# Loading the early pairs' kept first products into the raw-data buffers, two early pairs ahead

## The chip, the cores and the metric

The kernel runs on one core of one Trainium2 chip. The metric is the device time of one execution in microseconds (us). TensorE is called PE here, and its weight loads PEld. VectorE is DVE, ScalarE is ACT, GpSimd is POOL and SyncE is SP. SP issues all DMAs of this kernel, one after the other, from one queue that is worked off in order; its own rows are marked SPq.

## The reference, cut to what matters

One decoder layer runs over 16 meta tokens and 1024 real tokens with a width of 2048. Its first step is a large projection, and the change lies within it:

```python
hs = jnp.concatenate([meta, x], axis=1)          # (1, 1040, 2048)
h = rmsnorm(hs, gain)
zin = h @ w_in                                   # (1040, 2048) @ (2048, 10240)
q, k, v, g_attn, u, g_pool, m_attn, m_pool = jnp.split(zin, cuts, axis=-1)
# attention on q, k, v, times silu(g_attn); pooling of u, times silu(g_pool); both projected up,
# weighted by sigmoid(m_attn) and sigmoid(m_pool), summed, projected by w_out, added to x, normed
```

All inputs and the output are float32.

## The kernel before, in words

**Seven products instead of eight.** `w_in` is taken in 40 pairs of 128-column blocks (`duos`, a pair is called `d`). For each pair the product of a 2 x 2 arrangement of blocks (two halves of the 2048 rows by the two column blocks) with a 2 x 2 arrangement of activations (two halves of the width by two halves of the tokens) is made from seven block products. Four of them are made in the first phase, with the activation operands `X0`, `X1`, `X2` and `X3`, which lie in SBUF; the other three follow in a later phase. The first product (weights `c0` of the upper half by `X0`) is needed three times: `X1`'s product is added to it in PSUM and gives a finished output (`out_c`), and its value alone, `s1`, is subtracted from the accumulator `b` of `X2` and of `X3` (`out_nu` on line 260 and `out_up` on line 265, both on DVE).

**One product, in pieces.** `block` takes one product for one `kq` (half of a half's rows): 4 k-chunks by 3 matmuls of 128x128 by 128x512. The three matmuls (lines 138, 139, 140) are hi by hi, hi by lo and lo by hi, since every float32 operand is split into a high part `wh` and a low part `wl` by `op_of`: ACT makes `wh` (line 116), then DVE makes `wl` (line 117). There are four buffers of each. A product is two such blocks, 24 matmuls.

**Raw weights and their sums.** `all_raws` issues four loads of 512 KB for a pair: `raws[0][0]`, `raws[0][1]`, `raws[1][0]`, `raws[1][1]`. There is room for one pair's raw weights only, so a load waits until the pair before has been read. `make_sums` adds raw blocks on POOL (line 236), eight additions per pair: `r1`, `r2`, `r3`, `r4` for each `kq`. `r2` and `r3` become the operands of `X2` and `X3`; `r1` and `r4` are stored to DRAM (`d_r`, line 245) for the later phase. The addition that comes first on POOL in most pairs needs `raws[1][0]`.

**Early pairs and rest pairs.** While the tokens are normed and turned, only `X0` and `X1` exist, so the first six pairs (`early`) get their `X0` and `X1` products there, and `s1` is written to DRAM (`d_nu`). When `X2` and `X3` stand, `early_rest(d)` does what is left of an early pair: it loads its four raws, loads `s1` back (line 417), makes the sums, then `X2`, `out_nu`, `X3`, `out_up`. The 34 other pairs (`rest`) do all four products at a stretch: `X0`, `X2`, `X1`, `X3`. After each of the first rest pairs one early pair is inserted (`more`): early 0, rest 0, early 1, rest 1, and so on to early 5, rest 5, then rest pairs alone. I call an early pair with the rest pair behind it a round.

**What sets the order.** A scheduler sets each engine's order from the program. A tile of a pool comes with as many buffers as its tag has, and an instruction that writes a tile waits until the tile that had the buffer is read. `s1` of an early pair is a tile of tag `st`, which has four buffers (`STB`) and is also used for each pair's `out_c`, `out_nu` and `out_up`. Tiles of tag `wr` (four buffers, `wr_tile`) hold raw data in the early phase and again, in this phase, from the seventh rest pair on (`fetch_x22`).

Of the kernel before, what the change touches and what calls it, by code (L numbers as in the profile page):

```python
# [72 lines left out]
def trunk_kernel(  # L73
# [14 lines left out]
    nc = tc.nc  # L88
# [12 lines left out]
    def dtile(name, shape):  # L101
        return dram.tile(list(shape), F32, tag=name, name=name)
# [8 lines left out]
    def nm(s):  # L111
        uid[0] += 1
        return f"{s}_{uid[0]}"
# [50 lines left out]
    d_nu = [dtile(f"d_nu{n}", (P, HALF)) for n in range(ND)]  # L164
# [29 lines left out]
    with ExitStack() as actx:  # L194
# [3 lines left out]
        def acc_tile():  # L198
            return psA.tile([P, 512], F32, tag="acc", name=nm("acc"), bufs=4)
# [10 lines left out]
        with ExitStack() as xctx:  # L210
# [3 lines left out]
            def load_raw(d, kh, kq, pool=None):  # L214
                if pool is None:
                    raw = ws.tile([P, QD, 2 * P], F32, tag=f"raw{kh}", name=nm("raw"), bufs=2 - kh)
                else:
                    raw = pool.tile([P, QD, 2 * P], F32, tag="rawb", name=nm("raw"), bufs=1)
                rows = krows(kh, kq)
                for c, w in ((0, 2 * P),) if d.c1 == d.c0 + P else ((0, P), (P, P)):  # L220
                    col = d.c0 if c == 0 else d.c1
                    nc.sync.dma_start(raw[:, :, c : c + w], w_in[rows, col : col + w].rearrange("(k p) c -> p k c", p=P))
                return raw

            def c0(raw):
                return raw[:, :, :P]
# [21 lines left out]
            def st_tile(pool, bufs):  # L248
                return pool.tile([P, HALF], F32, tag="st", name=nm("st"), bufs=bufs)
# [8 lines left out]
            def out_nu(pool, bufs, d, s1, b):  # L258
                t = st_tile(pool, bufs)
                nc.vector.tensor_tensor(out=t, in0=s1, in1=b, op=ALU.subtract)  # L260
                nc.sync.dma_start(d_nu[d.n], t)
# [22 lines left out]
            early = ALL[:6]  # L284
            ops = {}

            def wr_tile():
                return wp.tile([P, 512], F32, tag="wr", name=nm("wr"), bufs=4)
# [7 lines left out]
            with tc.tile_pool(name="px", bufs=1, side="right", reuse_waits="tile") as px:  # L296
# [82 lines left out]
                s1 = wr_tile()  # L379
# [11 lines left out]
                for d in early[1:]:  # L391
# [4 lines left out]
                    s1 = wr_tile()  # L396
# [10 lines left out]
            wa = xctx.enter_context(tc.tile_pool(name="wa", bufs=1, side="right", reuse_waits="tile"))  # L407
            SB = {"r1": 2, "r2": 2, "r3": 2, "r4": 2}
            STB = 4

            def all_raws(d):
                return [[load_raw(d, 0, 0), load_raw(d, 0, 1)], [load_raw(d, 1, 0), load_raw(d, 1, 1, wa)]]

            def early_rest(d):
                raws = all_raws(d)
                s1 = st_tile(wa, STB)
                nc.sync.dma_start(s1, d_nu[d.n])
                r2, r3 = make_sums(wa, d, raws, SB)
                b = acc_tile()
                for kq in range(KQ):  # L420
                    block([b], WHOLE, X2, kq, op_of(r2[kq]), True)
                out_nu(wa, STB, d, s1, b)
                for kq in range(KQ):
                    block([b], WHOLE, X3, kq, op_of(r3[kq]), False)
                out_up(wa, STB, d, s1, b)
# [30 lines left out]
                nc.sync.dma_start(d_tm, tm.rearrange("p a q k c -> p (a q k c)"))  # L456

            rest = ALL[len(early) :]
            early_rest(early[0])
            raws = all_raws(rest[0])  # L460
            r2, r3 = make_sums(wa, rest[0], raws, SB)
            for n, d in enumerate(rest):
                pieces = WITHM if d.meta else WHOLE
                a, b = [acc_tile() for _ in pieces], acc_tile()
                for kq in range(KQ):
                    block(a, pieces, X0, kq, op_of(c0(raws[0][kq])), True)
                s1 = copy_p1(wa, STB, a, pieces)
                for kq in range(KQ):
                    block([b], WHOLE, X2, kq, op_of(r2[kq]), True)
                out_nu(wa, STB, d, s1, b)  # L470
                for kq in range(KQ):
                    block(a, pieces, X1, kq, op_of(c0(raws[1][kq])), False)
                out_c(wa, STB, d, a, pieces)
                m7 = [op_of(r3[kq]) for kq in range(KQ)]
                last = d is rest[-1]
                more = n + 1 < len(early)
                if not last and not more:
                    raws = all_raws(rest[n + 1])
                    r2, r3 = make_sums(wa, rest[n + 1], raws, SB)
                for kq in range(KQ):  # L480
                    block([b], WHOLE, X3, kq, m7[kq], False)
                out_up(wa, STB, d, s1, b)
                if more:
                    early_rest(early[n + 1])
                    raws = all_raws(rest[n + 1])
                    r2, r3 = make_sums(wa, rest[n + 1], raws, SB)
                if 7 <= n < 7 + KC // 2:
                    second_operands(n - 7)
                if n == 7 + KC // 2:
                    second_meta()  # L490
                if 6 <= n < 6 + KC // 2:
                    fetch_x22(n - 6)
# [101 lines left out]
        with ExitStack() as a0ctx:  # L594
# [37 lines left out]
            for g, win in enumerate(WINDOWS):  # L632
# [4 lines left out]
                d = named["u", g]  # L637
# [35 lines left out]
        with tc.tile_pool(name="a1", bufs=1, side="right", reuse_waits="tile") as a1:  # L673
# [127 lines left out]
            for h in range(HEADS):  # L801
                d = named["kv", h]
# [228 lines left out]
```

## Time and profile before

| what | us |
|---|---|
| median of 3 runs (2631.22 to 2642.57) | 2633.88 |
| the profiled execution | 2634.98 |
| its span, from the first to the last instruction in the trace | 2633.2 |

The profile is of one execution. Its times count from the start of the span. A row of a timeline gives the start, the duration, the engine, the line, the tiles (out<-in, without buffer numbers), how many equal instructions are merged (x2), and in brackets for how long the engine had been idle before and what ended that. A row of waits gives who waited for whom, the total, how many times, and the longest. A matmul's duration overlaps with the next one's, so 0.39 us stands for matmuls that start every 0.227 us. PEclk is the share of full clock that TensorE was granted in a stretch: 1.00 is 2.4 GHz, 0.50 is 1.2 GHz.

### The profile page before, as it was taken

Reading aid. Unit: us, or ns where it says so; the run is one execution under the profiler, and the core shown is the slowest. Engines: PE = TensorE matmul, PEld = TensorE weight load, DVE = VectorE, ACT = ScalarE, POOL = GpSimd, SP = SyncE. Lnnn points to the kernel's source line nnn. Section 1 sums busy time; section 2 is a strip of 40 time slices with the busy share of each in tenths; the row PEclk is TensorE's granted clock in tenths of the full one; section 3 lists DMA queues with packets and bytes.
Section 4 is the critical chain, followed back from the end, with each engine's and each line's share of the span. In section 5 each row is a group of like instructions: output and inputs, shape, how many; then the busy total and the mean of one; then the engine's idle time right before and its main releaser. Section 6 shows DMA issues by size and latency. Waiting matters only on the chain.

```text
span 2633.2 us, 36249 instructions
## 1 busy us (share of the span) xinstructions
PE 2506.8 (95%) x12968; PEld 2139.4 (81%) x12968; DVE 1279.7 (49%) x2121; ACT 933.9 (35%) x1893; POOL 871.0 (33%) x794
## 2 busy tenths in 40 slices
PE   6878789999999999899999999999989999999998
PEld 5767678888888887888888888888778888788888
DVE  5433235553333335565676567656644324544432
ACT  6412122222222225223555455545532224322331
POOL 1654455554444543224333333333111101211010
PEclk8989899999999999999999999999999999999999
DMA  5565555556555557434344433442384434664431
GB/s 178 166 205 188 176 184 196 193 207 203 175 182 178 185 174 242 143 117 152 118 123 137 127 118 124 137 127 90 117 275 144 143 108 138 192 199 141 147 102 64
DMA packets 392053, 415.88 MB, mean 158 GB/s; under 512 B 29872, under 2 KB 264752, under 8 KB 390832
## 3 DMA queue, kind: packets, MB, share of 16 engines
q1 hardware_dynamic: 391872, 413.57, 49.5%
q8 instruction: 101, 1.65, 0.3%
q14 instruction: 80, 0.66, 0.1%
HBM read 302.62 MB, written 110.85 MB: 157 GB/s over the span
## 4 chain that ended last, share of the span: by engine, by line
PE 79%; DVE 5%; DMA 3%; POOL 2%; issue 2%; ACT 1%; SPq 0%; POOLq 0%; DVEq 0%; ACTq 0%
PE acc L138 16%; PE acc L139 16%; PE acc L140 16%; PE accb L140 4%; PE accb L138 4%; PE accb L139 4%; PE accb L903 4%; PE accb L901 4%; PE accb L902 4%; POOL r L236 2%; PE tr L721 1%; DMA raw<-in_w_in_dram 1%; DVE s L649 1%; DVE bt L706 1%; PE av L139 1%
## 5 line engine op out<-in xcount | busy, mean ns | idle before, releaser
L138 PE MATMUL acc<-x,wh 128*128 128x512 f32 (+2 forms) x2736 | 983.8, 360 | 57.2 <-DVE st L260 42.0
L140 PE MATMUL acc<-x,wl 128*128 128x512 f32 (+2 forms) x2736 | 972.4, 355 | 2.3 <-POOL wl L117 1.3
L139 PE MATMUL acc<-x,wh 128*128 128x512 f32 (+2 forms) x2736 | 972.7, 356 | 0.0
L138 PEld LDWEIGHTS acc<-x,wh 128*128 128x128 f32 x2736 | 521.9, 191 | 126.9 <-DVE st L260 44.4
L140 PEld LDWEIGHTS acc<-x,wl 128*128 128x128 f32 x2736 | 520.8, 190 | 75.8 <-DVE wl L117 2.7
L139 PEld LDWEIGHTS acc<-x,wh 128*128 128x128 f32 x2736 | 521.8, 191 | 63.8
L116 ACT ACTIVATE wh<-wr 128x512 fp32r<-128x512 f32 x480 | 302.4, 630 | 523.2 <-PE acc L139 165.7
L117 DVE TENSOR_TENSOR wl<-wr,wh 128x512 fp32r<-128x512 f32 x360 | 257.4, 716 | 279.1 <-ACT wh L116 268.4
L117 POOL TENSOR_TENSOR wl<-wr,wh 128x512 fp32r<-128x512 f32 x120 | 166.5, 1387 | 346.4 <-ACT wh L116 282.1
L117 DVE TENSOR_TENSOR wl<-r,wh 128x512 fp32r<-128x512 f32 x160 | 147.0, 922 | 254.4 <-ACT wh L116 254.4
L116 ACT ACTIVATE wh<-r 128x512 fp32r<-128x512 f32 x160 | 100.9, 632 | 445.1 <-PE acc L139 234.5
L236 POOL TENSOR_TENSOR r<-raw,raw 128x512 f32<-128x512 f32 x80 | 110.5, 1381 | 403.9 <-DMA raw<-in_w_in_dram 376.4
L236 POOL TENSOR_TENSOR r<-r,raw 128x512 f32<-128x512 f32 x160 | 225.5, 1410 | 13.3 <-DMA raw<-in_w_in_dram 3.4
L138 PE MATMUL accb<-x,wh 128*128 128x512 f32 x512 | 200.9, 392 | 9.5 <-ACT wh L116 9.5
L140 PE MATMUL accb<-x,wl 128*128 128x512 f32 x512 | 201.0, 393 | 3.0 <-DVE wl L117 3.0
L139 PE MATMUL accb<-x,wh 128*128 128x512 f32 x512 | 200.6, 392 | 0.0
L117 DVE TENSOR_TENSOR wl<-raw,wh 128x512 fp32r<-128x512 f32 x136 | 115.4, 856 | 141.8 <-ACT wh L116 140.1
L903 PE MATMUL accb<-wl,x 128*128 128x512 f32 x448 | 174.4, 389 | 1.0 <-DVE wl L117 1.0
L901 PE MATMUL accb<-wh,x 128*128 128x512 f32 x448 | 174.3, 389 | 0.0
L902 PE MATMUL accb<-wh,x 128*128 128x512 f32 x448 | 174.3, 389 | 0.0
L116 ACT ACTIVATE wh<-raw 128x512 fp32r<-128x512 f32 x160 | 99.3, 627 | 186.2 <-PE acc L139 146.9
L705 DVE TENSOR_TENSOR_SCAN wt<-wt 128x272 f32<-128x272 f32 (+5 forms) x128 | 107.6, 840 | 110.5 <-POOL wt L700 65.1
(164 smaller groups left out, 2979.7 us busy)
## 6 DMA issues: line engine op xcount, KB each, us to landing
raw<-in_w_in_dram SPq DMA_DIRECT2D x96, 512.0 KB, 5.2
d_r<-r SPq DMA_DIRECT2D x160, 256.0 KB, 2.0
wr<-d_r SPq DMA_DIRECT2D x160, 256.0 KB, 2.9
raw<-in_w_in_dram SPq DMA_DIRECT2D x152, 256.0 KB, 5.2
wr<-in_w_out_dram SPq DMA_DIRECT2D x128, 256.0 KB, 2.6
wr<-in_w_in_dram SPq DMA_DIRECT2D x80, 256.0 KB, 3.0
wr<-in_w_pool_up_dram SPq DMA_DIRECT2D x64, 256.0 KB, 3.8
wr<-in_w_attn_up_dram SPq DMA_DIRECT2D x64, 256.0 KB, 3.5
```

The costliest lines, as they stand in the source:

```text
L116: nc.scalar.activation(hi, src, AF.Copy)
L117: (eng or nc.vector).tensor_tensor(out=lo, in0=src, in1=hi.bitcast(F32), op=ALU.subtract)
L138: nc.tensor.matmul(ps, wh, rh, start=first, stop=False, skip_group_check=skip)
L139: nc.tensor.matmul(ps, wh, rl, start=False, stop=False, skip_group_check=skip)
L140: nc.tensor.matmul(ps, wl, rh, start=False, stop=last, skip_group_check=skip)
L236: nc.gpsimd.tensor_tensor(out=t, in0=a, in1=b, op=ALU.add)
L649: nc.vector.tensor_tensor(out=nxt[:, lo:], in0=cur[:, lo:], in1=cur[:, lo - sh : TOK - sh], op=ALU.add)
L705: nc.vector.tensor_tensor_scan(out=rev, data0=rev, data1=rev, initial=wt[:, w : w + 1], op0=ALU.mult, op1=ALU.bypass)
L706: nc.vector.tensor_tensor(out=bt[:, :w], in0=bt[:, :w], in1=wt[:, 1 : w + 1], op=ALU.mult)
L901: nc.tensor.matmul(a, sh, wh, start=k == 0, stop=False)
L902: nc.tensor.matmul(a, sl, wh, start=False, stop=False)
L903: nc.tensor.matmul(a, sh, wl, start=False, stop=k == KC - 1)
```

## The change

`s1` of an early pair no longer comes from tag `st` and is no longer loaded within `early_rest`. A new function `fetch_s1` takes a `wr` tile and loads `s1` into it. It is called for early 0 and early 1 ahead of the first `early_rest`, and for early n + 2 ahead of `early_rest` of early n + 1.

```diff
+            kept = {}
+
+            def fetch_s1(d):
+                kept[d.n] = wr_tile()
+                nc.sync.dma_start(kept[d.n], d_nu[d.n])
+
             def early_rest(d):
                 raws = all_raws(d)
-                s1 = st_tile(wa, STB)
-                nc.sync.dma_start(s1, d_nu[d.n])
+                s1 = kept.pop(d.n)
                 r2, r3 = make_sums(wa, d, raws, SB)
...
             rest = ALL[len(early) :]
+            fetch_s1(early[0])
+            fetch_s1(early[1])
             early_rest(early[0])
...
                 if more:
+                    if n + 2 < len(early):
+                        fetch_s1(early[n + 2])
                     early_rest(early[n + 1])
```

Only SP's order changes. PE, ACT and POOL have the same instructions in the same order, and on DVE `out_nu` and `out_up` of early pairs read a `wr` tile where they read an `st` tile.

SP before, where `s1` of early 1 is loaded. `d_r7` are the sums of rest pair 1 (pair 7), `d_up6` is a result of rest pair 0, and `raw_336` and `raw_337` are the last two raws of rest pair 1:

```order
L222 DMA raw_336_1863<-in_w_in_dram 128x4x256
L279 DMA d_sa6_94<-st_304_1720 128x512
L222 DMA raw_337_1865<-in_w_in_dram 128x4x256
L245 DMA d_r7_0_141<-r1_340_1871 128x512
L245 DMA d_r7_1_142<-r4_341_1873 128x512
L266 DMA d_up6_253<-st_309_1755 128x512
L417 DMA st_314_1766<-d_nu1_208 128x512
L245 DMA d_r7_0_141<-r1_344_1881 128x512
```

SP after, the place where the same load (`d_nu1`) stands now, among the stores of the sums of early 0 (`d_r0`):

```order
L461 DMA d_tm_391<-tm2_974_5068 128x256
L418 DMA wr_252_1488<-d_nu0_207 128x512
L398 DMA d_nu5_212<-wr_244_1441 128x512
L418 DMA wr_253_1490<-d_nu1_208 128x512
L245 DMA d_r0_0_127<-r1_260_1504 128x512
```

The load has moved past all of rest pair 0 and out from behind two stores of rest pair 1's sums. The loads for early 2 to 5 stand as early: that of early 5 stands in round 2.

SP before, in round 1 (early 1 with rest 1), the stores of early 1's sums (`d_r1`) and the raws of rest 1 (`raw_334` to `raw_337`):

```order
L245 DMA d_r1_0_129<-r1_317_1772 128x512
L222 DMA raw_334_1859<-in_w_in_dram 128x4x256
L245 DMA d_r1_1_130<-r4_318_1774 128x512
L261 DMA d_nu6_213<-st_299_1685 128x512
L245 DMA d_r1_0_129<-r1_321_1782 128x512
L222 DMA raw_335_1861<-in_w_in_dram 128x4x256
L245 DMA d_r1_1_130<-r4_322_1784 128x512
L222 DMA raw_336_1863<-in_w_in_dram 128x4x256
```

SP after, the same place (the raws are `raw_335` to `raw_338` here):

```order
L245 DMA d_r1_0_129<-r1_318_1774 128x512
L418 DMA wr_427_2300<-d_nu4_211 128x512
L222 DMA raw_335_1861<-in_w_in_dram 128x4x256
L245 DMA d_r1_1_130<-r4_319_1776 128x512
L261 DMA d_nu6_213<-st_300_1687 128x512
L245 DMA d_r1_0_129<-r1_322_1784 128x512
L245 DMA d_r1_1_130<-r4_323_1786 128x512
L222 DMA raw_336_1863<-in_w_in_dram 128x4x256
L222 DMA raw_337_1865<-in_w_in_dram 128x4x256
```

In this one round the second raw of the rest pair now stands behind the last store of the early pair's sums; in the later rounds it stands ahead of that store, as before.

SP after, between the sums of rest 3 (`d_r9`) and the raws of early 4 (`raw_486` to `raw_489`). The same kinds stand there before the change, with one more load (`s1` of early 3) ahead of the last two `d_r9`:

```order
L245 DMA d_r9_0_145<-r1_461_2423 128x512
L245 DMA d_r9_1_146<-r4_462_2425 128x512
L222 DMA raw_486_2572<-in_w_in_dram 128x4x256
L261 DMA d_nu3_210<-st_445_2363 128x512
L222 DMA raw_487_2574<-in_w_in_dram 128x4x256
L266 DMA d_up3_250<-st_450_2398 128x512
L222 DMA raw_488_2576<-in_w_in_dram 128x4x256
L222 DMA raw_489_2578<-in_w_in_dram 128x4x256
```

Before and after, all four raws of an early pair stand behind the last store of the rest pair's sums.

## Rows read from the trace of the kernel before

**Rows 1.** The page, busy time of each engine.
```profile
PE 2506.8 (95%) x12968; PEld 2139.4 (81%) x12968; DVE 1279.7 (49%) x2121; ACT 933.9 (35%) x1893; POOL 871.0 (33%) x794
```
**Rows 2.** Waits of all engines, 140 to 360 us (total, times, longest).
```profile
DVE st L260 <- DMA st<-d_nu: 46.9, 5, 12.6
...
PE acc L138 <- DVE st L260: 42.0, 5, 12.2
```
**Rows 3.** Timeline of SP, 225 to 245 us.
```profile
226.29 0.32 SPq L245 DMA_DIRECT2D d_r<-r  x1
...
227.13 0.45 SPq L417 DMA_DIRECT2D st<-d_nu  x1
```
**Rows 4.** Timeline of DVE, 120 to 420 us: the second of five such waits.
```profile
230.44 0.69 DVE L260 TENSOR_TENSOR st<-st,acc 128x512 f32<-128x512 f32 x1 [8.02 <-DMA st<-d_nu]
```
**Rows 5.** Busy time by stretch after five waits: first, sum (PEclk third from the end).
```profile
188.51:194.71 6.20, 6.20 (x15) 4.84 (x16) 1.04 (x2) 0.63 (x1) 0.10 (x1) 0.50 0.81 244
...
sum 26.01, PE 25.99 PEld 20.49 DVE 4.42 ACT 1.30 POOL 0.89; mean PE 5.20 PEld 4.10 DVE 0.88 ACT 0.26 POOL 0.18
```
**Rows 6.** Timeline of POOL, 140 to 450 us: first addition of some pairs.
```profile
140.31 1.27 POOL L236 TENSOR_TENSOR r<-raw 128x512 f32<-128x512 f32 x1 [4.59 <-DMA raw<-in_w_in_dram]
...
161.37 1.29 POOL L236 TENSOR_TENSOR r<-raw,raw 128x512 f32<-128x512 f32 x1 [8.95 <-DMA raw<-in_w_in_dram]
178.34 1.26 POOL L236 TENSOR_TENSOR r<-raw,raw 128x512 f32<-128x512 f32 x1 [6.13 <-DMA raw<-in_w_in_dram]
...
264.64 1.30 POOL L236 TENSOR_TENSOR r<-raw,raw 128x512 f32<-128x512 f32 x1 [6.15 <-DMA raw<-in_w_in_dram]
289.66 1.28 POOL L236 TENSOR_TENSOR r<-raw,raw 128x512 f32<-128x512 f32 x1 [14.70 <-DMA raw<-in_w_in_dram]
...
306.56 1.29 POOL L236 TENSOR_TENSOR r<-raw,raw 128x512 f32<-128x512 f32 x1 [4.93 <-DMA raw<-in_w_in_dram]
331.20 1.29 POOL L236 TENSOR_TENSOR r<-raw,raw 128x512 f32<-128x512 f32 x1 [13.85 <-DMA raw<-in_w_in_dram]
...
348.61 1.29 POOL L236 TENSOR_TENSOR r<-raw,raw 128x512 f32<-128x512 f32 x1 [5.41 <-DMA raw<-in_w_in_dram]
374.54 1.28 POOL L236 TENSOR_TENSOR r<-raw,raw 128x512 f32<-128x512 f32 x1 [15.16 <-DMA raw<-in_w_in_dram]
...
396.97 1.29 POOL L236 TENSOR_TENSOR r<-raw,raw 128x512 f32<-128x512 f32 x1 [10.09 <-DMA raw<-in_w_in_dram]
...
419.63 1.29 POOL L236 TENSOR_TENSOR r<-raw,raw 128x512 f32<-128x512 f32 x1 [10.34 <-DMA raw<-in_w_in_dram]
441.31 1.33 POOL L236 TENSOR_TENSOR r<-raw,raw 128x512 f32<-128x512 f32 x1 [10.16 <-DMA raw<-in_w_in_dram]
```
**Rows 7.** Waits of the DMA queue, 160 to 375 us.
```profile
SPq L222 <- DVE wl L117: 21.3, 13, 2.3
```
**Rows 8.** Busy time by stretch: the first phase after the last early pair.
```profile
365.38:1000.00 634.62, 634.62 (x3331) 549.58 (x3330) 266.00 (x336) 175.90 (x332) 314.80 (x224) 1.00 0.57 187
```
**Rows 9.** Timeline of DVE, 388 to 398 and 724 to 729 us: `wl` from `r2`.
```profile
389.29 0.68 DVE L117 TENSOR_TENSOR wl<-r,wh 128x512 fp32r<-128x512 f32 x1
...
726.11 1.22 DVE L117 TENSOR_TENSOR wl<-r,wh 128x512 fp32r<-128x512 f32 x1 [3.87 <-ACT wh L116]
```
**Rows 10.** Timeline of PE: the matmuls that first read these two `wl`.
```profile
397.09 0.39 PE L140 MATMUL acc<-x,wl 128*128 128x512 f32 x1
...
728.69 0.39 PE L140 MATMUL acc<-x,wl 128*128 128x512 f32 x1
```
**Rows 11.** Timeline of PE, 100 to 420 us: two shorter waits.
```profile
125.79 0.50 PE L138 MATMUL acc<-x,wh 128*128 128x512 f32 x1 [2.48 <-ACT wr L397]
140.96 0.50 PE L138 MATMUL acc<-x,wh 128*128 128x512 f32 x1 [2.38 <-ACT wh L116]
```
**Rows 12.** Busy time by stretch, after these two waits.
```profile
126.45:129.86 3.41, 3.41 (x10) 2.64 (x9) 0.59 (x1) 0.63 (x1) 2.57 (x3) 0.50 0.37 127
140.96:147.00 6.04, 5.55 (x23) 4.08 (x24) 3.56 (x4) 1.26 (x2) 4.94 (x5) 1.00 0.78 273
```

## The prediction, made before the changed kernel ran

> **What bounds the kernel now.** I read the page first. PE is busy for 2506.8 us, 95% of the span [rows 1], so a change pays only where PE waits, or where its clock is down. The waits of 140 to 360 us come next: PE waits 42.0 us in 5 pieces for DVE's line 260, and DVE's line 260 waits 46.9 us in 5 pieces for the load `st<-d_nu` [rows 2]. It is one chain with five links, one in each of rounds 1 to 5; the kernel has no larger wait of PE for one reason. The timeline of SP shows why the load is late: it is issued at 227.13 us, right behind the store of the rest pair's result and behind a store of the next rest pair's sums [rows 3], and DVE starts `out_nu` at 230.44 after 8.02 us of idling [rows 4]. The wait has a second price. In the busy time by stretch, the work that follows each of the five waits runs at a granted clock of 0.50, that is 1.2 GHz, for 26.01 us together [rows 5]; at 2.4 GHz it would take half, so 13.0 us are lost. At stake are thus 42.0 + 13.0 = 55 us, 2.1% of the run.
>
> Then I asked what arrives next once PE is not held there, and went to POOL's timeline. The first additions of the pairs [rows 6] are the clock of a second chain: raw loads, eight additions, stores, raw loads. From early 1's sums (161.37) to rest 6's (374.54) five rounds take 213.17 us, 42.6 each. The first leg, from an early pair's sums to its rest pair's, takes 16.97, 16.90 and 17.41 us where both ends are shown, mean 17.1. The second leg takes the rest: 25.02, 24.64 and 25.93 us. PE's own work in a round is 144 matmuls; with one started every 0.227 us that is 32.7 us, less than any round of POOL. So PE has room to be held by POOL's chain, and that decides how much of the 55 us is kept.
>
> **The wait that is removed.** After the change all six loads stand far ahead: that of early 1 among the stores of early 0's sums, the others as early. `out_nu` reads an operand that has landed more than a pair before. The 46.9 us of DVE and the 42.0 us of PE [rows 2] go as such; I see no way in which this load could still be late, since its buffer has stood idle since the early phase.
>
> **What is late next.** An early pair's raws stand in SP's order behind the last store of the rest pair's sums, before and after, and its sums need them; that is the second leg. How much of its 25.5 us is due to the stalled PE? The raw buffers of the rest pair are read by `wh` and `wl` too, whose four buffers PE empties, and the DMA queue waits 21.3 us in 13 pieces for `wl` [rows 7]. These waits go when PE is on time. What is left is seen once, in round 0, where `s1` was loaded long before it was needed: from 140.31 to 161.37, 21.06 us, 8.95 of it idle for a raw [rows 6]. Built up from pieces: the eight additions take 12.0 us where DVE is at work beside them (289.66 to 306.56 less 4.93 idle), the raw burst adds 8.95, and one store more than in round 0 (`out_nu`'s rows now reach DRAM in each round) some 0.6, an estimate of about a quarter of the burst's time for 512 KB below: 21.6. The pairs without early pairs between them give legs of 22.43, 22.66 and 21.68 us (374.54, 396.97, 419.63, 441.31). I take 21.6, nearest to the one row of the same order; the bounds are 19.7 (the row of 21.06 with faster additions, next paragraph) and 22.7.
>
> A row speaks against this. While DVE stood still, the eight additions took 289.66 − 264.64 − 14.70 = 10.3 us; while it worked, 12.0. So part of the stall was not lost: POOL ran faster in it by 1.7 us per round. That is inside my 21.6; at the old speed the sum below would be 5 x 1.7 = 8.5 us better. The Trainium skill, "SBUF — State Buffer", section "Who interferes with whom", states the rule that a DVE instruction with two SBUF inputs contends with a GpSimd instruction that reads SBUF; by that rule the slower additions come back as soon as DVE works on, and the rows agree in direction.
>
> The first leg doesn't hang on PE: the early pair's raws and sums run while PE still works on the pair before. I keep 17.1; its bounds are the lowest and highest row, 16.9 and 17.4.
>
> **What is added.** Each fetch moves 256 KB that was moved before too; nothing is issued more often. But two fetches more (of early 3 and 4) fall within the raw loads of round 1, and in that round the second raw of rest 1 now stands behind the last store of early 1's sums. One more raw then lands in the burst: 512 KB at the 273 GB/s of the stretch 140.96 to 147.00 [rows 12] is 1.9 us. I take 2.0 for both, bounds 0 (the loads hide in POOL's additions) and 2.9 (with another 256 KB). DVE reads `wr` where it read `st`: I put nothing, since shape and type stay (0.69 us [rows 4]); were it twice as long, ten instructions would add 7 us to DVE, which is busy for 49% [rows 1] and covers them. The `st` buffer that is set free lets stores of results go a little earlier, which nobody waits for after the change; if somebody does, it is a gain inside the range.
>
> **The sum.** A round takes 17.1 + 21.6 = 38.7 us, five take 193.5, with 2.0 for round 1 195.5. Against 213.2 POOL's chain is 17.7 us ahead when it begins rest 6, at about 357 instead of 374.5. PE would be free to be further ahead: its 55 us exceed that. It is held to POOL, in waits for `wh` of `r2` early in `X2` of the early pair: 38.7 − 32.7 − the remaining idle for other operands, some 3 to 4 us a round, in place of 8.4.
>
> **What is given back later.** From 365.38 to 1000.00 PE isn't idle for a moment, 634.62 of 634.62 [rows 8]. POOL's chain is ahead of PE there, but not by much and not ever more. For rest 6 `wl` of `r2` is made at 389.97 (389.29 + 0.68 [rows 9]) and first read at 397.09 [rows 10]: 7.1 us to spare. For a pair further on it is made at 727.33 [rows 9] and read at 728.69 [rows 10]: 1.36 us, the least I found. After the change PE comes to rest 6 with no time to spare, so it will be held to POOL's chain all through this phase, and the end of the phase moves by POOL's lead plus what was to spare where it was least: 17.7 + 1.4 = 19. Some raw loads of the rest pairs waited on DVE and so on PE; with PE closer they start a little earlier. For that I put 1 us (bounds 0 and 9, the second of which belongs to the first rival). **The gain is 20 us.** The profiled execution took 2634.98 us, 1.8 more than its span and 1.1 more than the median of 2633.88. So 2615 for a repeat of that execution, and **2614** against the median.
>
> **Rivals.**
> *POOL's chain is not the bound.* If its second leg shrinks with PE all the way and the later pairs give back nothing, the gain grows to 17.7 + 9 = 27 us (2607), and in the extreme to all 55 us (2579). For it: the DMA queue waits 21.3 us for `wl`, on PE's side [rows 7], and in the stall the additions went faster. Against it: the leg of 21.06 us came with `s1` in place, and the spare time of 1.36 us at 728 us doesn't grow because PE arrives sooner. Chance 0.17, time about 2605.
>
> *POOL's chain is slower than the one row.* With legs of 17.4 and 22.7, as in the slowest rows [rows 6], a round takes 40.1; with another 0.6 for the store 40.7. Five of them and 2.0 are 205.5, the lead is 7.7, with 1.4 to spare 9 us: 2625. For it: round 0 had no rest pair's results to store ahead of its raws. Against it: 22.66 was seen while PE had the time to be late. Chance 0.20.
>
> *Slower than before, through the clock.* PE would come into the 28 rest pairs behind round 5 with a short wait in each. The wait of 2.48 us at 125.79 [rows 11] was followed by 3.41 us at a clock of 0.50 [rows 12], which costs 1.7 us beside the wait; the wait of 2.38 us at 140.96 [rows 11] was followed by a clock of 1.00 [rows 12]. If every one of the 28 pairs had such a drop, 28 x 1.7 = 48 us would outweigh the 20: 2662; in every second pair the loss is 24 and the time 2638. It decides from 12 drops on. Against it: the hold per pair in that phase is the difference between POOL's leg and PE's own work, 96 matmuls or 21.8 us for a rest pair: at most 22.66 − 21.8 = 0.9 us, below both waits shown. Chance 0.05, 0.04 of it over the bound of a measurement.
>
> *The change doesn't do what it says*, some load being late all the same through SP's order: 2634, no change. Chance 0.03.
>
> **How the numbers follow.** The forecast has 0.55, the first rival 0.17, the second 0.20, the clock 0.05, no effect 0.03. Within the forecast the unknown terms give: second leg 19.7 to 22.7 (five times 1.9 better or 1.1 worse), round 1's burst 2.0 better or 0.9 worse, later phase 1 worse or 8 better. They don't come together; 10 better and 6 worse is fair. The range takes in the second rival and the near part of the first: 2602 to 2627. About 0.5%, 13.2 us, is what a measurement of this kernel can tell from no change, so faster means below 2620.7. The forecast is nearly all below that, the second rival nearly all above. Faster 0.78, same 0.18, slower 0.04.
>
> **What would show it.** Step one is right if PE's waits for line 260 are gone or below 2 us, and the fetches are issued a round or more ahead. Step two is right if POOL's first additions stand 38 to 39.5 us apart from round to round, with rest 6's near 357 us, and if PE has new waits of 2 to 5 us a round for ACT's `wh` of `r2`. If those waits are missing and POOL's legs are shorter than 21, the first rival holds; legs over 22.5 speak for the second. The later phase should show many small waits of PE, under 1 us each, at a clock of 1.00; a clock of 0.50 there is the third rival. The eight additions should take 12.0 us in the second leg also. A wait that I haven't seen, on another queue, would make all of it wrong: then PE's waits from 140 to 360 us would name another releaser.

## The result, and the profile after

The changed kernel takes 2604.58 us (median of 4 runs, 2601.93 to 2607.19) against 2633.57 us of the kernel before (median of 4). The ratio is 0.9884, 95% interval [0.9858, 0.9909]: 29 us faster, between 24 and 37. The forecast of 2614 us was 9 us too slow; the measured time lies inside the range, where the first rival stood (2605). The profiled execution took 2601.93 us with a span of 2600.2, 33.0 us less than the span before; that pair of executions lies somewhat further apart than the medians do.

The page, busy time of each engine, to hold against [rows 1]: PE has about as much work in a shorter span.

```profile
PE 2502.7 (96%) x12968; PEld 2132.8 (82%) x12968; DVE 1279.1 (49%) x2121; ACT 930.7 (36%) x1893; POOL 873.3 (34%) x794
```

Waits of the changed kernel from 140 to 360 us (total, times, longest), to hold against [rows 2]:

```profile
DVE st L260 <- PE acc L140: 16.1, 11, 1.8
PE acc L138 <- ACT wh L116: 13.5, 7, 3.6
```

DVE's wait for `st<-d_nu` and PE's wait for line 260 are gone from the list. What DVE's line 260 waits for now is PE, as it should be. PE's new wait is for `wh`, 13.5 us in 7 pieces, one of which, 3.6 us, lies ahead of the rounds: 9.9 us in 6 pieces are left for them.

The reason is seen in two rows of early 1: SP's timeline has the load at 126.71 us, ahead of all of rest pair 0, and DVE's has `out_nu` at 176.01 us, behind a wait for PE alone (compare [rows 4]).

```profile
126.71 0.42 SPq L418 DMA_DIRECT2D wr<-d_nu  x1
```
```profile
176.01 0.69 DVE L260 TENSOR_TENSOR st<-wr,acc 128x512 f32<-128x512 f32 x1 [0.77 <-PE acc L140]
```

POOL's timeline, first additions of early 1, rest 1, early 4, rest 4, early 5, rest 5 and rest 6, as in [rows 6]:

```profile
161.44 1.29 POOL L236 TENSOR_TENSOR r<-raw,raw 128x512 f32<-128x512 f32 x1 [8.55 <-DMA wr<-d_nu]
179.06 1.28 POOL L236 TENSOR_TENSOR r<-raw,raw 128x512 f32<-128x512 f32 x1 [6.78 <-DMA raw<-in_w_in_dram]
...
277.23 1.29 POOL L236 TENSOR_TENSOR r<-raw,raw 128x512 f32<-128x512 f32 x1 [9.74 <-DMA raw<-in_w_in_dram]
294.16 1.29 POOL L236 TENSOR_TENSOR r<-raw,raw 128x512 f32<-128x512 f32 x1 [6.13 <-DMA raw<-in_w_in_dram]
314.89 1.28 POOL L236 TENSOR_TENSOR r<-raw,raw 128x512 f32<-128x512 f32 x1 [9.74 <-DMA raw<-in_w_in_dram]
331.29 1.38 POOL L236 TENSOR_TENSOR r<-raw,raw 128x512 f32<-128x512 f32 x1 [5.62 <-DMA raw<-in_w_in_dram]
351.97 1.29 POOL L236 TENSOR_TENSOR r<-raw,raw 128x512 f32<-128x512 f32 x1 [9.63 <-DMA raw<-in_w_in_dram]
```

(The first row names the load of an `s1` as releaser, which is no operand of that addition; its idle time is near the 8.95 us of [rows 6].) Five rounds take 351.97 − 161.44 = 190.5 us instead of 213.2. The forecast had 195.5 and rest 6 at about 357.

Now the same two places in the later phase as in [rows 9] and [rows 10]: PE's matmuls that first read `wl` of `r2`, for rest 6 and rest 21, and DVE's instructions that made it.

```profile
366.02 0.39 PE L140 MATMUL acc<-x,wl 128*128 128x512 f32 x1
```
```profile
697.62 0.39 PE L140 MATMUL acc<-x,wl 128*128 128x512 f32 x1
```
```profile
362.59 1.22 DVE L117 TENSOR_TENSOR wl<-r,wh 128x512 fp32r<-128x512 f32 x1 [3.86 <-ACT wh L116]
...
695.04 1.22 DVE L117 TENSOR_TENSOR wl<-r,wh 128x512 fp32r<-128x512 f32 x1 [3.87 <-ACT wh L116]
```

This is the surprise. PE reads 397.09 − 366.02 = 31.07 us earlier for rest 6, and 728.69 − 697.62 = 31.07 us earlier for rest 21, to the hundredth the same. Nothing was given back. The time to spare is 366.02 − 363.81 = 2.2 us for rest 6, where it was 7.1, and 697.62 − 696.26 = 1.36 us for rest 21, the very value of before. The many small waits of PE that the prediction named as a sign are not there. The busy time by stretch says the same: from 344 to 965 us PE is never idle and its clock is 1.00 (third number from the end), as in [rows 8].

```profile
344.00:965.00 621.00, 621.00 (x3271) 538.20 (x3270) 261.34 (x327) 168.98 (x323) 314.44 (x224) 1.00 0.59 192
```

So 31 of the 33 us come from the rounds. The other 2 lie elsewhere in the run, where nothing was changed, and I did not follow them.

### The profile page after: what moved, and what is told of

The parts are those of the page before. It is cut to its first block, busy times and chain, and to the rows that moved or that the text cites. A ratio compares the mean times of both kernels' runs of the same rounds, so it can differ in the third digit from the quotient of the medians.

```text
span 2600.2 us, 36248 instructions
## 1 busy us (share of the span) xinstructions
PE 2502.7 (96%) x12968; PEld 2132.8 (82%) x12968; DVE 1279.1 (49%) x2121; ACT 930.7 (36%) x1893; POOL 873.3 (34%) x794
## 4 chain that ended last, share of the span: by engine, by line
PE 82%; DVE 5%; DMA 3%; POOL 3%; issue 1%; ACT 1%; SPq 0%; POOLq 0%; DVEq 0%; ACTq 0%
PE acc L138 17%; PE acc L140 17%; PE acc L139 17%; PE accb L912 4%; PE accb L911 4%; PE accb L910 4%; PE accb L140 4%; PE accb L138 4%; PE accb L139 4%; POOL r L236 2%; DMA raw<-in_w_in_dram 2%; PE tr L730 1%; DVE s L658 1%; DVE wl L117 1%; DVE bt L715 1%
## 5 line engine op out<-in xcount | busy, mean ns | idle before, releaser
L138 PEld LDWEIGHTS acc<-x,wh 128*128 128x128 f32 x2736 | 520.1, 190 | 96.6 <-ACT wh L116 22.4
L902 POOL TENSOR_TENSOR sa<-sa,sp 128x512 f32<-128x512 f32 x32 | 50.9, 1590 | 324.8 <-DVE sa L901 324.8
```

What stands on the lines that cost most here:

```text
L138: nc.tensor.matmul(ps, wh, rh, start=first, stop=False, skip_group_check=skip)
L902: nc.gpsimd.tensor_tensor(out=sa, in0=sa, in1=sps.pop(c), op=ALU.add)
```

## The experiments

Times are medians; a ratio is that to the kernel before on the same chip. In the texts on record the theories are named A and B anew for each run.

### One late load put back

```diff
             def early_rest(d):
                 raws = all_raws(d)
-                s1 = kept.pop(d.n)
+                if d.n == 3:
+                    s1 = st_tile(wa, STB)
+                    nc.sync.dma_start(s1, d_nu[d.n])
+                else:
+                    s1 = kept.pop(d.n)
...
-                    if n + 2 < len(early):
+                    if n + 2 < len(early) and n + 2 != 3:
                         fetch_s1(early[n + 2])
```

> The changed kernel, but early 3 alone loads s1 in the old way (st tile, at its turn). Theory A, a delay of TensorE in the rounds is kept to the end, since POOL's raw-and-sums chain follows TensorE in the later phase: in round 3 TensorE waits 7 to 12 us for line 260 and then runs some 5 us at half clock, the waits for wh of r2 in that round (1.8 us and its half clock of 1.7) go, so TensorE comes to rest 6 some 7 us later than in the changed kernel and stays as much later up to 960 us: about 2612 us. Theory B, the reasoning of the prediction, POOL's chain sets the end of the phase: TensorE's delay is taken up by its spare time at rest 6 and the least spare time near 700 us shrinks by nothing; the end moves only by POOL's own delay, 0 to 3 us: about 2606 us.

Measured: 2610.44 us, ratio 0.9904 [0.9882, 0.9926], 5.9 us above the changed kernel. One wait is back (waits of 140 to 360 us):

```profile
DVE st L260 <- DMA st<-d_nu: 12.7, 1, 12.7
PE acc L138 <- DVE st L260: 12.3, 1, 12.3
```

PE reads the same operands of rest 6 and rest 21 at

```profile
373.73 0.39 PE L140 MATMUL acc<-x,wl 128*128 128x512 f32 x1
```
```profile
705.33 0.39 PE L140 MATMUL acc<-x,wl 128*128 128x512 f32 x1
```

that is 7.71 us later than in the changed kernel at both places. Theory A holds: a delay of the rounds stays in the time to the end. Of the 7.71 us, 2.7 were there ahead of the rounds, where nothing differs: PE's row at 141.00 us of the changed kernel stands at 143.71 here. So about 5 us come from the one load, near the 5.9 of the medians. Its 12.3 us and their half clock are more than that, so a part did come back, but within the rounds: from 150 us on PE waits for `wh` 6.0 us in 4 pieces, where the changed kernel has 9.9 in 6.

### The clock by itself

The kernel before, with work for PE in the waits:

```diff
+            FILL = 30
...
+                if d.n:
+                    z = psA.tile([P, 512], F32, tag="z", name=nm("fill"), bufs=2)
+                    for i in range(FILL):
+                        nc.tensor.matmul(z, X2[0][0][:, 0, :P], X2[0][0][:, 0, :HALF], start=i == 0, stop=i == FILL - 1)
                 out_nu(wa, STB, d, s1, b)
```

> The kernel before, with 30 matmuls of no use (128x128 by 128x512, into a PSUM tile that nobody reads, 26 and 4 of them apart in round 1) between X2 and X3 of early 1 to 5, so that TensorE works during most of each wait for line 260. Theory A, 13 us of what was at stake are the clock: the stretches at half clock behind the five waits go, TensorE still waits for what is left of each (in sum about 9 us), it comes to rest 6 about 10 to 12 us earlier and keeps that: about 2622 us. Theory B, what TensorE wins is held by POOL's chain or by the load, whose place in SP's order does not change: under 3 us, about 2632 us. A rival to both: the useless matmuls delay more than they win, 2635 us or more.

Measured: 2632.44 us (10 runs, 2627.16 to 2643.02), ratio 0.9993 [0.9978, 1.0007]. The total can't tell. The trace can: DVE still waits 44.5 us for the load, PE now waits 11.5 for line 260, and it reads for rest 6 at 391.49 and for rest 21 at 723.09, 5.60 us before 397.09 and 728.69.

```profile
DVE st L260 <- DMA st<-d_nu: 44.5, 5, 12.5
...
PE acc L138 <- DVE st L260: 11.5, 5, 6.2
```
```profile
391.49 0.39 PE L140 MATMUL acc<-x,wl 128*128 128x512 f32 x1
```
```profile
723.09 0.39 PE L140 MATMUL acc<-x,wl 128*128 128x512 f32 x1
```

So a wait that is kept busy does give back a part of the 13.0 us, with the loads as late as before. The clock itself shows more than the 5.60 us. In rounds 2 to 5, where the kernel before ran 26.01 − 6.20 = 19.8 us at 0.50 [rows 5] and lost 9.9 by it, this one runs at 1.00 throughout (third number from the end):

```profile
194.20:375.00 180.80, 175.53 (x771) 144.10 (x771) 60.35 (x72) 38.38 (x64) 92.38 (x68) 1.00 0.58 186
```

The half clock behind the wait of round 1 is left (187.30 to 194.10 at 0.50, PE busy for 5.01 us). A part of the 9.9 us is spent again: five times 30 matmuls at 0.227 us are 34.0 us, by estimate, and with the 11.5 us of waits they take 3.5 more than the 42.0 before.

### More work for POOL in the later phase

In two kernels, of which the second has `range(2)`:

```diff
                     r1 = add("r1", c1(raws[0][kq]), c1(raws[1][kq]))
+                    if kq == 0 and d.n >= 12:
+                        for _ in range(1):
+                            nc.gpsimd.tensor_tensor(out=r1, in0=c1(raws[0][kq]), in1=c1(raws[1][kq]), op=ALU.add)
```

> The changed kernel with one addition on POOL done twice (r1 of kq 0) in each of the 28 rest pairs from rest 6 on, 1.3 us each. Theory A, POOL's own leg is 20.7 us (as the last rounds of the changed kernel show it) and TensorE's pace there 21.8 to 22.2: one addition more makes 22.0, which TensorE hardly feels, 0 to 4 us in all, about 2607 us. Theory B, the legs of 21.7 to 22.7 that the kernel before showed are POOL's own, with 1.4 us to spare at the least: 28 times 1.3 less 1.4 is 35 us, about 2640 us.

> The same with the addition done three times, 2.6 us more in each of the 28 pairs. Theory A: a leg of 23.3 us against TensorE's 22.2 costs 1.1 us in each pair, 28 to 31 us in all, about 2634 us, and TensorE then waits in nearly each pair for wh of r2. Theory B: 28 times 2.6 less 1.4 is 71 us, about 2676 us.

Measured: 2634.07 us with one addition more (+29.5 against the changed kernel) and 2668.97 with two (+64.4). Here my new theory A fell, and B, the view of the prediction, was nearly right (+35 and +71). From rest 7 to rest 33 POOL's first additions run from

```profile
375.59 1.29 POOL L236 TENSOR_TENSOR r<-raw,raw 128x512 f32<-128x512 f32 x1 [9.31 <-DMA raw<-in_w_in_dram]
```
```profile
976.58 1.29 POOL L236 TENSOR_TENSOR r<-raw,raw 128x512 f32<-128x512 f32 x1 [9.60 <-DMA raw<-in_w_in_dram]
```

601.0 us for 26 pairs, 23.1 a pair. Take away the added 1.3: POOL's own leg is 21.8 us. (With two additions more the same places are 376.51 and 1014.02 us, 24.5 a pair; less 2.6 that is 21.9.) PE's pace from rest 6 to rest 21 is (697.62 − 366.02) / 15 = 22.1. POOL has 0.3 us a pair in hand, and no more. In the kernel with two additions more PE waits for `wh` up to 2.3 us at a time in this phase, and five stretches of 3.41 us there, the first from 416.11 us, run at a clock of 0.50: what the third rival describes does occur, with a slower POOL than the changed kernel has.

### PE made late once

If POOL's own leg is 21.8 us, why does [rows 6] show 22.4 and 22.7?

```diff
+                if n == 6:
+                    z = psA.tile([P, 512], F32, tag="z", name=nm("fill"), bufs=2)
+                    for i in range(36):
+                        tc.keep_in_program_order(nc.tensor.matmul(z, X2[0][0][:, 0, :P], X2[0][0][:, 0, :HALF], start=i == 0, stop=i == 35))
                 for kq in range(KQ):
                     block([b], WHOLE, X2, kq, op_of(r2[kq]), True)
```

> The changed kernel with 36 matmuls of no use (8.2 us, into a PSUM tile that nobody reads) once, ahead of X2 of rest 6. It tells why the later phase gave nothing back. Theory A, POOL's chain is held by TensorE as soon as it is more than some 2 us ahead, since its raw loads wait for buffers that wl sets free: TensorE is 8.2 us later from rest 6 to 960 us, the time to spare of r2's second wl rises to about 7 us at once and is down to 1.3 to 2 us again near rest 21, where POOL is 8 us later than in the changed kernel; about 2612 us. Theory B, POOL's chain runs at its own pace whatever TensorE does: POOL's additions of rest 21 start within 2 us of the changed kernel's 684.6 us and the time to spare there is about 8 us more, 9 to 10 us; TensorE as late as under A, about 2612 us. The place of POOL's additions tells them apart, not the total.

Measured: 2610.36 us. DVE's `wl` of `r2` and PE's reading of it, for rest 6 and rest 21:

```profile
362.78 1.22 DVE L117 TENSOR_TENSOR wl<-r,wh 128x512 fp32r<-128x512 f32 x1 [3.86 <-ACT wh L116]
...
700.76 1.22 DVE L117 TENSOR_TENSOR wl<-r,wh 128x512 fp32r<-128x512 f32 x1 [2.40 <-ACT wh L116]
```
```profile
374.48 0.39 PE L140 MATMUL acc<-x,wl 128*128 128x512 f32 x1
```
```profile
706.08 0.39 PE L140 MATMUL acc<-x,wl 128*128 128x512 f32 x1
```

PE is 8.46 us late at both places. The time to spare jumps to 374.48 − 364.00 = 10.5 us and is down to 706.08 − 701.98 = 4.1 at rest 21. POOL's additions of rest 21, in the changed kernel and in this one:

```profile
684.59 1.56 POOL L236 TENSOR_TENSOR r<-raw,raw 128x512 f32<-128x512 f32 x1 [11.39 <-DMA raw<-in_w_in_dram]
```
```profile
689.67 1.30 POOL L236 TENSOR_TENSOR r<-raw,raw 128x512 f32<-128x512 f32 x1 [11.15 <-DMA raw<-in_w_in_dram]
```

POOL is 5.1 us later though no addition was put in there (two of one pair changed places): more than B's 2, less than A's 8 by then. So POOL does slow down when it is ahead of PE. Where this happens is in the waits of the DMA queue. Of the kernel before (380 to 700 us), of the changed one and of this one (320 us each from the same place on):

```profile
SPq L222 <- DVE wl L117: 18.9, 20, 2.8
```
```profile
SPq L222 <- DVE wl L117: 5.5, 18, 1.0
```
```profile
SPq L222 <- DVE wl L117: 13.8, 19, 2.3
```

The loads of raws (line 222) wait until `wl` has read the raw buffers, and `wl` waits for buffers that PE sets free. With PE late that costs 18.9 or 13.8 us, with PE on time 5.5.

### The early load without the free buffer

```diff
             def fetch_s1(d):
-                kept[d.n] = wr_tile()
+                kept[d.n] = st_tile(wa, STB)
```

> The changed kernel, but the fetches go into tiles of tag st (four buffers, shared with the results) and not into wr: the loads come as far ahead as in the changed kernel, and two of the four st buffers are held by s1 that waits for its use. Theory A, only the time of the load matters: DVE's 46.9 us of waits for the load go, about 2605 us. Theory B, the buffer matters: s1, out_c, out_nu and out_up of a rest pair share two buffers, DVE and ACT wait for stores of results that stand behind stores of sums on SP, TensorE waits for them in each round, 2615 to 2640 us.

Measured: 2606.20 us, ratio 0.9898 [0.9873, 0.9923], the same as the changed kernel. The price that B named exists, but it takes the place of another wait: PE waits 12.1 us in 4 pieces for ACT's line 255, which waits for an `st` buffer, where it waited for `wh`. What counts is when the load comes. (The other half, `wr` without the two early pairs of lead, is no other kernel: with `fetch_s1(d)` written in `early_rest(d)` itself, every engine has the same rows in the same order as the changed kernel. The scheduler draws a load forward as soon as its buffer is free.)

```profile
PE acc L138 <- ACT st L255: 12.1, 4, 3.5
```

### What bounds the rounds now

Five kernels worked at the waits for `wh` that are left. First, X3 ahead of X2 in the early pairs:

```diff
-                b = acc_tile()
+                e, b = acc_tile(), acc_tile()
+                for kq in range(KQ):
+                    block([e], WHOLE, X3, kq, op_of(r3[kq]), True)
+                up = st_tile(wa, STB)
+                nc.vector.tensor_tensor(out=up, in0=e, in1=s1, op=ALU.subtract)
                 for kq in range(KQ):
                     block([b], WHOLE, X2, kq, op_of(r2[kq]), True)
                 out_nu(wa, STB, d, s1, b)
-                for kq in range(KQ):
-                    block([b], WHOLE, X3, kq, op_of(r3[kq]), False)
-                out_up(wa, STB, d, s1, b)
+                nc.vector.tensor_tensor(out=up, in0=up, in1=b, op=ALU.add)
+                nc.sync.dma_start(d_up[d.n], up)
```

> The changed kernel with X3 ahead of X2 in each early pair (out_up is made in two steps on DVE, since X3 gets an accumulator of its own): r3 needs one raw and one addition, r2 two raws and two additions, so TensorE's first operand of an early pair is there sooner. Theory A, POOL's chain of raws and sums (16.8 + 21.4 us a round in the changed kernel against 32.7 us of matmuls) bounds the rounds: the waits move from the first product to the second, TensorE comes to rest 6 within 4 us of the changed kernel, about 2604 us. Theory B, the order of the operands bounds them: TensorE's 13 us of waits in the rounds and 7 us of clock behind them go for the most part, 2585 to 2592 us.

Measured: 2590.99 us, ratio 0.9837 [0.9812, 0.9863], 13.6 us better than the changed kernel and the lowest median of all. B's time, but which of its reasons? In this kernel POOL's order changed too: the scheduler puts `r3` of both `kq`, which need raws 0 and 1 alone, ahead of the other additions in the rest pairs of rounds 1 to 5, while the early pairs of rounds 2 to 5 begin as before. So the second kernel changes POOL's order alone, with the additions of the six early pairs (`d.n < 6`) kept in the order written (`r3`, `r3`, then `r2`, `r1`, `r4` for each `kq`); the scheduler then puts those of the six rest pairs between them in the same order. PE, DVE and ACT are as in the changed kernel. The third does both.

```diff
+                ahead = d.n < 6
...
-                    nc.gpsimd.tensor_tensor(out=t, in0=a, in1=b, op=ALU.add)
+                    i = nc.gpsimd.tensor_tensor(out=t, in0=a, in1=b, op=ALU.add)
+                    if ahead:
+                        tc.keep_in_program_order(i)
...
-                for kq in range(KQ):
-                    r3.append(add("r3", c0(raws[0][kq]), c1(raws[0][kq])))
+                if ahead:
+                    for kq in range(KQ):
+                        r3.append(add("r3", c0(raws[0][kq]), c1(raws[0][kq])))
+                for kq in range(KQ):
+                    if not ahead:
+                        r3.append(add("r3", c0(raws[0][kq]), c1(raws[0][kq])))
                     r2.append(add("r2", r3[kq], c1(raws[1][kq])))
```

> The changed kernel with POOL's additions of the round pairs in another order: r3 of both kq first (they need raws 0 and 1 alone), then r2, r1, r4 of kq 0, then of kq 1; TensorE, DVE and ACT keep their order. Theory A, what made the kernel with X3 first quicker in the rounds (34.5 us a round in place of 38.1) is that two additions move into POOL's wait for the last two raws, so that its chain is shorter: a round of 34 to 35.5 us here too, TensorE's waits for wh of r2 down by half or more, 2588 to 2594 us. Theory B, it was TensorE's need for r3 in place of r2: no more than 4 us here, 2600 to 2606 us.

> Both: X3 ahead of X2 in the early pairs, and POOL's additions in that order in all round pairs. Theory A, the two take the same waits away, the rest of them lies in the raws: within 4 us of X3 first alone, 2587 to 2593 us. Theory B, they add up until TensorE's own 32.7 us a round are reached: the 1.9 us a round that were left go, 2579 to 2585 us.

Measured: 2593.85 us, ratio 0.9853 [0.9826, 0.9879], and 2595.00, ratio 0.9852 [0.9829, 0.9874]. POOL's order alone gains 10.7 us, and the two don't add up; the three intervals overlap, so which of the three kernels is quickest is not shown. POOL's timeline, first additions of early 4 and early 5 with POOL's order changed (line 238 is line 236 there), and the same with X3 first:

```profile
266.59 1.29 POOL L238 TENSOR_TENSOR r<-raw 128x512 f32<-128x512 f32 x1 [5.46 <-DMA raw<-in_w_in_dram]
...
301.14 1.29 POOL L238 TENSOR_TENSOR r<-raw 128x512 f32<-128x512 f32 x1 [5.35 <-DMA raw<-in_w_in_dram]
```
```profile
267.73 1.28 POOL L236 TENSOR_TENSOR r<-raw,raw 128x512 f32<-128x512 f32 x1 [9.83 <-DMA raw<-in_w_in_dram]
...
302.24 1.28 POOL L236 TENSOR_TENSOR r<-raw,raw 128x512 f32<-128x512 f32 x1 [9.75 <-DMA raw<-in_w_in_dram]
```

A round is 34.5 us in both, where the changed kernel has 314.89 − 277.23 = 37.7. So the chain of raws and sums was a bound of the rounds, and POOL's wait for the third raw a part of it: the idle time ahead of the first addition falls from 9.74 to 5.46 us when that addition needs only the first raw.

The last two were to shorten the chain in other ways and were slower:

```diff
-                def add(tag, a, b):
+                def add(tag, a, b, eng=nc.gpsimd):
...
-                    nc.gpsimd.tensor_tensor(out=t, in0=a, in1=b, op=ALU.add)
+                    eng.tensor_tensor(out=t, in0=a, in1=b, op=ALU.add)
...
-                    r4 = add("r4", r2[kq], c0(raws[1][kq]))
+                    r4 = add("r4", r2[kq], c0(raws[1][kq]), nc.vector if d.n < 12 else nc.gpsimd)
```

> The changed kernel with two of the eight additions (r4 of both kq) of the first twelve pairs on DVE instead of POOL. Theory A, POOL's chain bounds the rounds: its additions take 8 us instead of 10.9, each leg is shorter by up to 2.7 us, a round falls from 38.1 to 33 to 35 us, TensorE's waits for wh go for the most part and it comes to rest 6 12 to 20 us earlier, 2585 to 2593 us. Theory B, the raw loads bound the rounds, not the additions: under 4 us, 2601 to 2606 us. A rival: DVE in order waits for raws and makes wl late, slower than 2608 us.

```diff
-                        nc.sync.dma_start(d_r[d.n][m][:, kq * 512 : (kq + 1) * 512], r.rearrange("p k c -> p (k c)"))
+                        (nc.scalar if d.n < 12 else nc.sync).dma_start(d_r[d.n][m][:, kq * 512 : (kq + 1) * 512], r.rearrange("p k c -> p (k c)"))
```

> The changed kernel with the stores of the sums r1 and r4 of the first twelve pairs issued by ACT, so that SP does not wait for POOL ahead of the next pair's raw loads (149.5 us in 39 waits from 160 to 375 us in the changed kernel). Theory A, the place of the early pairs' raws behind the last store of sums is a part of the second leg of 21.4 us: raws 0 and 1 load while POOL still adds, the leg shortens by 2 to 5 us, 10 to 20 us in all, 2585 to 2595 us. Theory B, the raws wait for their buffers, which the last additions set free anyway: under 3 us, 2602 to 2606 us. A rival: ACT waits for POOL ahead of wh, slower than 2608 us.

Measured: 2631.06 us, ratio 0.9985 [0.9966, 1.0004], and 2625.58, ratio 0.9971 [0.9956, 0.9985]. In both the rival won. Waits from 140 to 360 us, with `r4` on DVE and with the stores on ACT:

```profile
DVE r L236 <- POOL r L236: 84.3, 22, 7.4
...
PE acc L140 <- DVE wl L117: 38.0, 6, 8.3
```
```profile
PE acc L138 <- ACT wh L116: 40.1, 7, 8.8
```

An instruction that waits for POOL was put into the order of an engine that PE needs for `wl` or `wh`, and PE then waits 38 to 40 us for these, nearly the 42.0 of before, where the changed kernel waits 13.5 for `wh` and 3.6 for `wl`. With the stores on ACT it looks like this: a `wh` that is made from a raw and needs nothing of POOL's stands behind a store of sums and waits 3.64 us for POOL.

```profile
227.17 0.33 ACTq L245 DMA_DIRECT2D d_r<-r  x1
227.59 0.63 ACT L116 ACTIVATE wh<-raw 128x512 fp32r<-128x512 f32 x1 [3.64 <-POOL r L236]
```

## Why the prediction was right, and where not

**The wait that is removed: right.** The 42.0 us of PE and 46.9 us of DVE are gone, and the loads come more than a pair early. `st_ahead` shows that the time of the load is the cause, `early3_old` that the load of early 3 alone is worth 5 to 6 us; the other four were not put back one by one.

**What is late next: right in kind, the size near.** PE waits for `wh` of `r2`, 9.9 us in the rounds in place of 42.0. First legs measured 17.62, 16.93 and 16.40 us where 17.1 was taken, second legs 20.73 (294.16 to 314.89) and 20.68 where 21.6 was. Rest 6's sums start at 351.97, 22.6 us ahead of before, where the sum had 17.7: 5 us too little, spread over ten legs. One reason given for the slow second leg did not hold: the additions were to take 12.0 us with DVE at work, a figure read from a first leg. From 294.16 to 314.89 less 9.74 they took 11.0 us, with DVE at work: between the 10.3 and the 12.0 of before. In the first leg ahead of it they took 294.16 − 277.23 − 6.13 = 10.8. The direction is that of the rule which the prediction cites, the Trainium skill, "SBUF — State Buffer", section "Who interferes with whom". But of the eight additions from 294.16 on only one was slow; it began while DVE made a `wl`, from 298.77 to 299.99 us, and the seven others took 1.3 us each:

```profile
299.40 1.75 POOL L236 TENSOR_TENSOR r<-raw,raw 128x512 f32<-128x512 f32 x1
```

The 0.6 us put for one store more is not the quarter of 1.9 us that it is called, which is 0.5; nothing hangs on it.

**What is given back later: the step that failed.** The prediction held PE to POOL's chain all through the later phase. It let PE keep POOL's lead at rest 6 plus the least time to spare, 17.7 + 1.4, and put 1 us, bounds 0 and 9, for raw loads that start earlier when PE is not late. Measured: POOL's chain never held PE there. PE kept all of its 31.07 us, and POOL's lead grew to 715.65 − 684.59 = 31.1 us at rest 21 (the first number is that addition before the change):

```profile
715.65 1.57 POOL L236 TENSOR_TENSOR r<-raw,raw 128x512 f32<-128x512 f32 x1 [11.62 <-DMA raw<-in_w_in_dram]
```

So the term of 1 us was 31.1 − 22.6 = 8.5 us. I had read the legs of 22.43 and 22.66 us as POOL's own pace. They were POOL held back by a late PE, as the DMA queue's 18.9, 5.5 and 13.8 us and `pe_late` show. And the 1.36 us to spare, which I wanted to spend, is no reserve: it comes out again in the changed kernel, because POOL only runs ahead of PE until its raws wait for PE's buffers. The sum with both terms as measured, 22.6 + 8.5 + 0, is 31.1 us, what the trace has at 700 us. Both misses go the same way. That 2604.58 us lies inside the range owes something to luck: the range took in the near part of the first rival, whose 9 us for this term are what came.

**The rivals.** The first one has the time, 2605 us, and half of the mechanism: the later phase gives nothing back. Its other half fails, since POOL's chain does bound the rounds (the kernel with POOL's order changed gained 10.7 us by that alone). The later phase gives nothing back because POOL's own leg there is 21.8 us against PE's 22.1, a margin so thin that one addition of 1.3 us a pair cost 29.5 us. The second rival's legs above 22.5 us did not appear in the rounds. The third, half clock in the later phase, is excluded by the 1.00 from 344 to 965 us. Round 1's burst (2.0 us) is not shown: from 161.44 to the first addition of early 2 it took 39.8 us, where the last two rounds took 37.7 and 37.1, but round 2, in which no raw changed its place, took 240.26 − 201.20 = 39.1. POOL's row of early 2:

```profile
201.20 1.28 POOL L236 TENSOR_TENSOR r<-raw,raw 128x512 f32<-128x512 f32 x1 [11.19 <-DMA raw<-in_w_in_dram]
```

**Clock and waits.** The half clock is not gone in the changed kernel, but smaller. Rounds 2 to 5 have one stretch of 3.41 us at 0.50 each; the one of round 2 is shown in the last section, the others are

```profile
250.73:254.14 3.41, 3.11 (x8) 2.04 (x7) 3.24 (x5) 1.63 (x4) 0.29 (x1) 0.50 0.90 268
288.27:291.68 3.41, 3.05 (x7) 2.47 (x8) 2.71 (x5) 1.11 (x3) 0.00 (x0) 0.50 0.88 261
325.82:329.23 3.41, 2.96 (x7) 2.38 (x8) 2.80 (x5) 1.20 (x3) 0.00 (x0) 0.50 0.85 263
```

PE is busy for 12.5 us in the four, which costs 6.3 us. So 13.0 − 6.3 = 6.7 us of the clock were won. PE's waits from 143 to 344 us are

```profile
PE acc L138 <- ACT wh L116: 9.9, 6, 1.8
PE acc L140 <- DVE wl L117: 3.6, 9, 0.5
```

so 42.0 − 13.5 = 28.5 us of waits were won.

**What stays open.** The two together are 35.2 us, 4 more than the 31.07 that PE is ahead. I did not follow the difference.

## What to carry to other kernels

Where an engine is busy without a break, the pace of a chain beside it is no proof of what that chain can do: it may be held back by the very engine that it feeds. Slow it a little, or delay the engine once, and see which of the two moves. Where a second chain limits a loop after a wait is gone, look at which input its first instruction needs, since an order that needs fewer of them may be the next gain.

## What the hardware showed that I had not expected

Waits shorter than the 2.48 us of [rows 11] were followed by half clock. In round 2 of the changed kernel PE waited 1.69 us and then 1.83 us for `wh`, with two waits of 0.4 to 0.5 us for `wl` between and behind:

```profile
205.78 0.50 PE L138 MATMUL acc<-x,wh 128*128 128x512 f32 x1 [1.69 <-ACT wh L116]
...
211.30 0.50 PE L138 MATMUL acc<-x,wh 128*128 128x512 f32 x1 [1.83 <-ACT wh L116]
```
```profile
213.18:216.59 3.41, 3.41 (x10) 2.63 (x9) 1.71 (x3) 0.44 (x2) 0.00 (x0) 0.50 0.89 234
```

The stretch behind them ran at a clock of 0.50 (third number from the end), while a wait of 2.38 us in the kernel before, with one of 0.49 us soon behind it, had gone by without it ([rows 11] and [rows 12]). The length of one wait alone is not what decides.
